# GpSimd in place of VectorE for the low halves of pieces 1 to 14 of the weights

## The chip, the cores and the metric

The kernel runs on one core of one Trainium2 chip. The metric is the time of one execution in device microseconds; three runs of the kernel before took 2193.1, 2188.76 and 2193.03 us, median 2193.03. The engines are named as in the profile: PE is TensorE (matmul), PEld its weight load, DVE is VectorE, ACT is ScalarE, POOL is GpSimd, SP is SyncE, which here issues most of the transfers.

## The reference, cut to what matters

One decoder layer over 512 positions of width 2048: adaLN modulation from a conditioning vector c, an input projection, an S5 mixer beside a dilated attention, an output projection and a SwiGLU channel mixer, in float32. The change lies in the first part:

```python
mod = (silu(c) @ w_mod + b_mod)                 # 6 blocks of 2048
h = rmsnorm(x, g_mix) * (1.0 + sc1) + sh1       # [512, 2048]
proj = h @ w_in                                 # [512, 4096] = u, q, k, v
```

## The kernel before

**Splits.** TensorE multiplies in fp32r. Each float32 operand is split in two: the high half is the value cast to fp32r, the low half is the value minus its high half. A product is three matmuls (`mm3`, lines 190 to 193): high by high, low by high and high by low. For weights a *piece* is 128 rows (one k tile) by 1024 columns of a matrix: SyncE loads it into `raw` (`load_piece`, 5 buffers), ScalarE casts it to `hi` (`split_piece`, line 161), and VectorE subtracts for `lo` (`split_lo`, line 165); `hi` and `lo` have 3 buffers each. A piece gives TensorE 24 matmuls: 8 blocks of 128 columns, 3 matmuls each, with a moving operand of 512 positions.

**Activations.** For each k tile, `h_make` forms the modulated input: VectorE multiplies (line 518, two halves of 256 positions), ScalarE adds the shift and casts to the high half (line 519, `hA` for k below 4 and `hB` above), VectorE forms the low half (line 523). It needs the modulation of tile k first: `gv` multiplies four 128x1024 parts of `w_mod` by the conditioning vector `cb` on VectorE (line 314, with an accumulated sum), and `h_mod` (lines 504 to 508) turns the sums into `gs` and `mod`. The parts of `w_mod` come through SyncE as well (`mraw`, 8 buffers in this phase).

**Order.** A list `prog` holds three products at the start: 4 pieces with k = 0 to 3 (partial q and k), 6 pieces with k = 0 to 5 (more of q and k), and 16 pieces with k = 0 to 15 (u). Pieces are counted through: 0 to 3, 4 to 9, 10 to 25. `run` walks the list; `need(i)` sees that pieces up to i are split, one or two ahead of TensorE; `pump` advances background work, among it `head_rest`, which makes the activations for k from 4 on. Each engine has one queue and works through it in order; the framework orders each queue by a priority, and splits have a raised one (`tc.high_priority(30)`). An instruction that waits holds all behind it on its engine. On SyncE the load of piece n+5 waits until piece n's `raw` has been read, and the loads of `mraw` queue behind it.

GpSimd has five small rows at the program's start and three transfers later; the first of these (`Kd<-s5z`, line 641) come at 182.9 us. All other splits, in the second half of the kernel too, are formed by ScalarE and VectorE.

## Time and profile before

| what | value |
|---|---|
| median of three runs | 2193.03 us |
| profiled execution, its own time | 2189.05 us |
| its span | 2187.2 us |
| PE busy | 2109.8 us (96%) |
| DVE busy | 1516.8 us (69%) |
| ACT busy | 849.6 us (39%) |
| POOL busy | 2.0 us, 7 instructions |
| L165, all low halves of weight pieces on DVE | 192 instructions, mean 1221 ns |
| L161, their high halves on ACT | 192 instructions, mean 1052 ns |

PE's share is near full over the whole span, but the first stages differ: there PE starts at 33.45 us and has gaps until 60 us. A busy share of a whole span therefore doesn't say what one of these stages is bound by. In the rows of a timeline the first number is the start, the second the duration; brackets give the idle time of the engine just before and what ended it. Starts of successive rows of one engine can lie closer than the duration, since instructions overlap at their ends. PEclk is the granted TensorE clock, 1.00 being full speed.

### The profile page before, as it was taken

The numbers are of one execution on the slowest core, as the hardware profiler recorded it, in microseconds if no ns is written. First come the engines' busy times: TensorE is split into PE (matmuls) and PEld (weight loads), VectorE is DVE, ScalarE is ACT, GpSimd is POOL, SyncE is SP. The second block draws the span as 40 slices with busy tenths as digits, with TensorE's granted clock in tenths as the row PEclk, the third lists the DMA queues.
The fourth block names the chain that finished last, engine by engine and source line by source line (L and its number), as shares of the span: only waits on it lengthen the run. The fifth ranks groups of instructions, "written<-read, shape, count | busy, mean of one in ns | idle before, by whom it ended". The sixth has DMA issues, their size and how long they took to land.

```text
span 2187.2 us, 32392 instructions
## 1 busy us (share of the span) xinstructions
PE 2109.8 (96%) x12800; PEld 1874.8 (86%) x12800; DVE 1516.8 (69%) x2216; ACT 849.6 (39%) x1209; POOL 2.0 (0%) x7
## 2 busy tenths in 40 slices
PE   6999999889999999999999999999999999999996
PEld 4778787767787778999999999999999888888885
DVE  7896886986888776687887888878887543242224
ACT  3432343257753253444444444444444111121111
POOL 0000000000000000000000000000000000000000
PEclk9999988999999999999999999999999999999998
DMA  9999785768887633343343333434435999655552
GB/s 344 339 357 174 215 248 197 238 210 296 299 284 249 219 114 97 130 144 123 135 138 132 128 135 131 143 123 136 138 132 217 323 320 327 204 195 194 193 173 77
DMA packets 212047, 435.92 MB, mean 199 GB/s; under 512 B 50676, under 2 KB 87924, under 8 KB 211896
## 3 DMA queue, kind: packets, MB, share of 16 engines
q1 hardware_dynamic: 211656, 433.13, 59.8%
q8 instruction: 101, 1.65, 0.3%
q0 software_dynamic: 240, 0.72, 0.1%
q14 instruction: 50, 0.41, 0.1%
HBM read 380.38 MB, written 53.41 MB: 198 GB/s over the span
## 4 chain that ended last, share of the span: by engine, by line
PE 73%; DVE 8%; DMA 3%; issue 1%; ACT 0%; DVEq 0%; SPq 0%; ACTq 0%
PE g L191 11%; PE g L193 11%; PE g L192 11%; PE y L1436 5%; PE y L1437 5%; PE y L1438 5%; PE z L1437 3%; PE x L1437 3%; PE x L1436 3%; PE z L1436 3%; PE x L1438 3%; PE z L1438 3%; DMA mraw<-in_w_mod 3%; DVE mraw L314 1%; DVE lo L165 1%
## 5 line engine op out<-in xcount | busy, mean ns | idle before, releaser
L165 DVE TENSOR_TENSOR lo<-raw,hi 128x1024 fp32r<-128x1024 f32 x192 | 234.2, 1221 | 323.8 <-ACT hi L161 323.7
L161 ACT CAST hi<-raw 128x1024 fp32r<-128x1024 f32 x192 | 201.6, 1052 | 557.4 <-PE g L192 356.3
L1167 ACT CAST hi<-raw 128x1024 fp32r<-128x1024 f32 x176 | 185.1, 1052 | 292.5 <-PE x L1437 125.4
L314 DVE SCALAR_TENSOR_TENSOR mraw<-mraw,cb 128x1024 f32<-128x1024 f32 x192 | 232.1, 1219 | 75.8 <-DMA mraw<-in_w_mod 75.6
L1169 DVE TENSOR_TENSOR lo<-raw,hi 128x1024 fp32r<-128x1024 f32 x176 | 215.1, 1223 | 90.2 <-ACT hi L1167 90.1
L191 PE MATMUL g<-f,hi 128*128 128x512 f32 x704 | 273.9, 389 | 0.0
L192 PE MATMUL g<-f,hi 128*128 128x512 f32 x704 | 273.9, 389 | 0.0
L193 PE MATMUL g<-f,lo 128*128 128x512 f32 x704 | 273.9, 389 | 0.0
L1167 ACT CAST hi<-s 128x1024 fp32r<-128x1024 f32 x120 | 126.3, 1053 | 165.0 <-PE y L1437 82.8
L1436 PE MATMUL y<-t,hi 128*128 128x256 f32 x640 | 179.8, 281 | 0.0
L1437 PE MATMUL y<-t,hi 128*128 128x256 f32 x640 | 179.8, 281 | 0.0
L1438 PE MATMUL y<-t,lo 128*128 128x256 f32 x640 | 179.8, 281 | 0.0
L1437 PE MATMUL x<-b,hi 128*128 128x256 f32 x640 | 179.8, 281 | 0.0
L1436 PE MATMUL x<-b,hi 128*128 128x256 f32 x640 | 179.8, 281 | 0.0
L1438 PE MATMUL x<-b,lo 128*128 128x256 f32 x640 | 179.8, 281 | 0.0
L1169 DVE TENSOR_TENSOR lo<-s,hi 128x1024 fp32r<-128x1024 f32 x120 | 146.5, 1221 | 16.3 <-ACT hi L1167 15.7
L193 PEld LDWEIGHTS g<-f,lo 128*128 128x128 f32 x704 | 132.1, 188 | 27.5
L191 PEld LDWEIGHTS g<-f,hi 128*128 128x128 f32 x704 | 132.1, 188 | 27.4
L192 PEld LDWEIGHTS g<-f,hi 128*128 128x128 f32 x704 | 132.1, 188 | 27.3
L191 PE MATMUL g<-hB,hi 128*128 128x512 f32 x288 | 115.6, 403 | 12.8 <-DVE rt L901 12.8
L1436 PEld LDWEIGHTS x<-b,hi 128*128 128x128 f32 x640 | 120.6, 188 | 0.0
L1437 PEld LDWEIGHTS x<-b,hi 128*128 128x128 f32 x640 | 120.6, 188 | 0.0
(321 smaller groups left out, 4935.4 us busy)
## 6 DMA issues: line engine op xcount, KB each, us to landing
mraw<-in_w_mod SPq DMA_DIRECT2D x192, 512.0 KB, 6.0
raw<-in_w_down SPq DMA_DIRECT2D x88, 512.0 KB, 3.9
f<-fd SPq DMA_DIRECT2D x88, 512.0 KB, 4.2
raw<-in_w_gate SPq DMA_DIRECT2D x80, 512.0 KB, 3.3
raw<-in_w_up SPq DMA_DIRECT2D x80, 512.0 KB, 3.8
raw<-in_w_in SPq DMA_DIRECT2D x64, 512.0 KB, 5.2
fd<-fo SPq DMA_DIRECT2D x40, 512.0 KB, 4.5
raw<-in_w_out SPq DMA_DIRECT2D x32, 512.0 KB, 5.4
```

The source lines that it names most:

```text
L161: ACT.copy(hi, p["raw"])
L165: tt(p["hl"][1], p["raw"], p["hl"][0].bitcast(F32), op=ALU.subtract)
L191: PE.matmul(ps, lhs[0], rhs[0], start=first, stop=False)
L192: PE.matmul(ps, lhs[0], rhs[1], start=False, stop=False)
L193: PE.matmul(ps, lhs[1], rhs[0], start=False, stop=last)
L314: stt(raw, raw, 1.0, cb[:, h * (D // 2):(h + 1) * (D // 2)], op0=ALU.mult, op1=ALU.mult, accum_out=macc[:, m, h:h + 1])
L1167: ACT.copy(hi, raw)
L1169: tt(lo, raw, hi.bitcast(F32), op=ALU.subtract)
L1436: PE.matmul(o, hi[:, sl], bh[:, k], start=f, stop=False, skip_group_check=True)
L1437: PE.matmul(o, hi[:, sl], bo[:, k], start=False, stop=False, skip_group_check=True)
L1438: PE.matmul(o, lo[:, sl], bh[:, k], start=False, stop=l, skip_group_check=True)
```

## The change

For pieces 1 to 14 of the first program the subtraction of the low half is issued on GpSimd; piece 0 and pieces from 15 on stay on VectorE. Before the second program (the channel mixer's last product) the limit is set to 0, so that nothing moves there.

```diff
     prog, pieces = [], []
+    LP = 14
     at = [0, 1, 0]
...
     def split_lo(p):
-        tt(p["hl"][1], p["raw"], p["hl"][0].bitcast(F32), op=ALU.subtract)
+        e = POOL if 0 < p["n_"] <= LP else DVE
+        e.tensor_tensor(p["hl"][1], p["raw"], p["hl"][0].bitcast(F32), op=ALU.subtract)
...
             with tc.high_priority(30):
+                pieces[at[0]]["n_"] = at[0]
                 split_lo(pieces[at[0]])
...
     prog.clear()
     pieces.clear()
+    LP = 0
     at[:] = [0, 0, 0]
```

Line numbers of the changed kernel are 2 or 3 higher here (165 becomes 167, 314 becomes 317, 518 becomes 521, 523 becomes 526).

VectorE's queue between the modulation of k=2 and the activations of k=3, before the change. `lo_344`, `lo_396`, `lo_448` and `lo_524` are the low halves of pieces 1 to 4, `st_413` belongs to k=2, `mraw_347` and those after it to k=3:

```order
L508 TENSOR_TENSOR gs<-gs,gb_164 128x1
L165 TENSOR_TENSOR lo_344<-raw_289,hi_343 128x1024
L518 SCALAR_TENSOR_TENSOR st_413<-vg,gs,rbc 128x256 x2
L165 TENSOR_TENSOR lo_396<-raw_291,hi_395 128x1024
L523 SCALAR_TENSOR_TENSOR hA_106<-st_413,mod,hA_105 128x256 x2
L165 TENSOR_TENSOR lo_448<-raw_293,hi_447 128x1024
L165 TENSOR_TENSOR lo_524<-raw_295,hi_523 128x1024
L314 SCALAR_TENSOR_TENSOR mraw_347,macc<-mraw_347,cb 128x1024
L314 SCALAR_TENSOR_TENSOR mraw_350,macc<-mraw_350,cb 128x1024
```

The same place of VectorE's queue in the changed kernel:

```order
L511 TENSOR_TENSOR gs<-gs,gb_164 128x1
L521 SCALAR_TENSOR_TENSOR st_413<-vg,gs,rbc 128x256 x2
L526 SCALAR_TENSOR_TENSOR hA_106<-st_413,mod,hA_105 128x256 x2
L317 SCALAR_TENSOR_TENSOR mraw_347,macc<-mraw_347,cb 128x1024
L317 SCALAR_TENSOR_TENSOR mraw_350,macc<-mraw_350,cb 128x1024
```

The four subtractions are gone from between the activations of k=2 and the modulation of k=3. GpSimd's queue before the change, from its last constant to the end:

```order
L1559 MEMSET const-uint8-127 128x1
L1565 UNCONDITIONAL_BRANCH
L641 DMA Kd<-s5z 112x512 x2
L1010 DMA mask<-in_km 128x512
L1565 UNCONDITIONAL_BRANCH
```

And in the changed kernel, from the same constant; the low halves of pieces 6 to 14 follow in the same form, and then the two transfers to `Kd`:

```order
L1563 MEMSET const-uint8-127 128x1
L1569 UNCONDITIONAL_BRANCH
L167 ISA
L167 TENSOR_TENSOR lo_344<-raw_289,hi_343 128x1024
L167 TENSOR_TENSOR lo_396<-raw_291,hi_395 128x1024
L167 TENSOR_TENSOR lo_448<-raw_293,hi_447 128x1024
L167 TENSOR_TENSOR lo_524<-raw_295,hi_523 128x1024
L167 TENSOR_TENSOR lo_530<-raw_306,hi_529 128x1024
```

The fourteen subtractions stand on GpSimd's queue now, behind one new ISA row. Each waits for its cast on ScalarE and, from piece 3 on, for TensorE to have left its buffer. On ScalarE's queue the casts of pieces 1 to 5 and of pieces 12 to 14 keep their places among the activations: the cast of piece 5 ahead of the activation of k=3, the cast of piece 13 behind three activations of k=7 and 8. On SyncE's queue the order stays, and the loads of pieces 6 to 19 wait for GpSimd's reading of the buffer where they waited for VectorE's.

## The prediction

> **What bounds the kernel now.** I read the stages first, then what TensorE waited for, then the rows of the engines that it waited for. The stages (busy time of each engine in six stretches):

> ```profile
> core 0: us, PE busy (x) PEld busy (x) DVE busy (x) ACT busy (x) POOL busy (x), PEclk, DMA share, GB/s
> 33.45:60.00 26.55, 20.29 (x75) 15.02 (x76) 24.95 (x51) 8.06 (x12) 0.00 (x0) 0.94 0.99 373
> 60.00:115.00 55.00, 55.00 (x236) 45.33 (x236) 46.76 (x112) 22.99 (x39) 0.00 (x0) 0.97 0.94 336
> 115.00:120.00 5.00, 3.84 (x16) 2.57 (x15) 5.00 (x9) 3.29 (x5) 0.00 (x0) 1.00 0.89 339
> 120.00:200.00 80.00, 80.00 (x355) 66.09 (x354) 75.18 (x174) 25.82 (x37) 1.19 (x2) 1.00 0.89 294
> ```

> The change ends with piece 14, whose low half is made at 118 us. From 60 us on TensorE is full, but for 1.16 us in 115 to 120; before that it is idle for 6.26 us while VectorE works for 24.95 of 26.55 us. So a faster VectorE can win back about 7.4 us and what the clock adds, and every microsecond that VectorE loses in these 85 us is near a gate of TensorE. TensorE's rows after a wait, in its timeline (start, duration, and in brackets the idle time and its releaser):

> ```profile
> 45.10 0.96 PE L193 MATMUL g<-hA,lo 128*128 128x512 f32 x3 [2.35 <-DVE lo L165]
> 58.60 1.22 PE L191 MATMUL g<-hA,hi 128*128 128x512 f32 x2 [3.67 <-ACT hA L519]
> 65.98 0.39 PE L191 MATMUL g<-hA,hi 128*128 128x512 f32 x1
> 116.05 0.50 PE L191 MATMUL g<-hA,hi 128*128 128x512 f32 x1 [0.27 <-ACT hi L161]
> 117.67 0.50 PE L193 MATMUL g<-hA,lo 128*128 128x512 f32 x1 [0.89 <-DVE lo L165]
> ```

> The first wait is for piece 1's low half, the second for the activations of k=3, the last two for piece 13. Piece 3 runs from 58.60 to 65.98, 7.38 us; the clock says why:

> ```profile
> 58.00:64.00 6.00, 5.40 (x13) 4.04 (x14) 5.93 (x12) 2.30 (x5) 0.00 (x0) 0.52 0.91 345
> 64.00:70.00 6.00, 6.00 (x28) 4.95 (x27) 3.06 (x5) 3.68 (x6) 0.00 (x0) 1.00 0.56 209
> ```

> After the wait of 3.67 us the granted clock was 0.52 for 6 us. By the stage from 120 to 200 a matmul takes 80/355 = 0.225 us at full clock, a piece of 24 takes 5.4 us, and the slow stretch cost 7.38 - 5.4 = 2.0 us. After the wait of 2.35 us three matmuls lasted 0.96 us, after the longer one two lasted 1.22: the shorter wait left the clock full.

> VectorE's timeline, with the low halves (L165) of pieces 1 to 5, then 6 to 12, and the rows that gate TensorE:

> ```profile
> 41.19 1.22 DVE L314 SCALAR_TENSOR_TENSOR mraw<-mraw,cb 128x1024 f32<-128x1024 f32 x1
> 43.81 1.23 DVE L165 TENSOR_TENSOR lo<-raw,hi 128x1024 fp32r<-128x1024 f32 x1
> 45.75 1.22 DVE L165 TENSOR_TENSOR lo<-raw,hi 128x1024 fp32r<-128x1024 f32 x1
> 47.68 1.22 DVE L165 TENSOR_TENSOR lo<-raw,hi 128x1024 fp32r<-128x1024 f32 x1
> 50.43 1.23 DVE L165 TENSOR_TENSOR lo<-raw,hi 128x1024 fp32r<-128x1024 f32 x1 [1.53 <-ACT hi L161]
> 51.57 1.22 DVE L314 SCALAR_TENSOR_TENSOR mraw<-mraw,cb 128x1024 f32<-128x1024 f32 x1
> 57.39 0.21 DVE L506 SCALAR_TENSOR_TENSOR mod<-macc,vec 128x1 f32<-128x1 f32 x1
> ...
> 84.08 1.23 DVE L165 TENSOR_TENSOR lo<-raw,hi 128x1024 fp32r<-128x1024 f32 x1 [1.31 <-ACT hi L161]
> 89.52 1.22 DVE L165 TENSOR_TENSOR lo<-raw,hi 128x1024 fp32r<-128x1024 f32 x1 [0.25 <-ACT hi L161]
> 96.47 1.22 DVE L165 TENSOR_TENSOR lo<-raw,hi 128x1024 fp32r<-128x1024 f32 x1
> 100.36 1.22 DVE L165 TENSOR_TENSOR lo<-raw,hi 128x1024 fp32r<-128x1024 f32 x1
> 113.23 0.88 DVE L518 SCALAR_TENSOR_TENSOR st<-vg,gs,rbc 128x256 f32<-128x256 f32 x2
> ```

> From the start at 50.43 to the next at 51.57 is 1.14 us: that is what a low half occupies of VectorE. And ScalarE's timeline, the casts to the high halves (L161) and the activations (L519):

> ```profile
> 39.80 1.98 ACT L161 CAST hi<-raw 128x1024 fp32r<-128x1024 f32 x2
> 46.29 1.03 ACT L161 CAST hi<-raw 128x1024 fp32r<-128x1024 f32 x1
> 54.74 1.04 ACT L161 CAST hi<-raw 128x1024 fp32r<-128x1024 f32 x1 [4.34 <-PE g L192]
> 57.64 0.91 ACT L519 ACTIVATE hA<-st,mod 128x256 fp32r<-128x256 f32 x2 [1.85 <-DVE mod L506]
> 77.74 1.05 ACT L161 CAST hi<-raw 128x1024 fp32r<-128x1024 f32 x1 [8.60 <-PE g L192]
> 78.69 1.31 ACT L519 ACTIVATE hB<-st,mod 128x256 fp32r<-128x256 f32 x3
> 113.75 1.31 ACT L519 ACTIVATE hB<-st,mod 128x256 fp32r<-128x256 f32 x3 [7.55 <-DVE st L518]
> 114.96 1.04 ACT L161 CAST hi<-raw 128x1024 fp32r<-128x1024 f32 x1
> ```

> **Gate 1** is the activation of k=3: VectorE's L506 at 57.39, ScalarE to 58.55, TensorE at 58.60. **Gate 2** is piece 13: its cast at 114.96 stands in ScalarE's queue behind activations that wait until VectorE's L518 at 113.23.

> **The change part by part.** VectorE loses 14 low halves, 14 x 1.14 = 16.0 us, all before 118 us. GpSimd gets them. Its queue was empty there (the page's busy tenths in 40 slices, then rows from the answers on `Kd` and of the timeline):

> ```profile
> POOL 0000000000000000000000000000000000000000
> L641 POOL DMA_DIRECT2D Kd<-s5z x2: 539/598/656, 182.9 to 183.5; - x2
> 182.87 1.22 DVE L314 SCALAR_TENSOR_TENSOR mraw<-mraw,cb 128x1024 f32<-128x1024 f32 x1
> ```

> The new queue starts with an ISA row that waits for nothing; it has 40 us until piece 1 and costs nothing. The two transfers behind the 14 rows, at 182.9, are 60 us clear of the last of them.

> How long does one of the 14 take there? No row has GpSimd at arithmetic on a tile. The nearest are the cast that reads one operand of the same size (39.80: 1.98 for two, 1.0 each) and VectorE's subtraction, 1.22. Both operands read one after the other is two such reads, 2.0 to 2.44. Below 1.0 nothing points, and above 5.4, a piece of TensorE, GpSimd could not keep up at all. I take 2.3, near two VectorE reads, since a subtraction has two operands. [...]

> The second unknown weighs more: how much of that time VectorE must stand still. Call it h. Almost all of VectorE's work beside these rows reads two operands from SBUF too (L314: mraw and cb; L518 and L523 as well). The one overlap in the trace, GpSimd's transfer at 182.9 beside L314 at 182.87 with its usual 1.22 us, reads no tile by GpSimd's arithmetic and says nothing. So h lies between 0 (side by side; less can't be) and 2.44 (in turns). I take turns, h = 2.3: two engines with the same two streams from the same tiles, and nothing in the trace that shows such streams beside each other.

> [...]

> *Gate 1.* Before 57.39 VectorE made pieces 1 to 4, 4 x 1.14 = 4.56, and stood 1.53 for piece 4's cast: 6.1 us go. Added are GpSimd's rows of pieces 1 to 5, whose casts end between 40.8 (just before VectorE's L314 at 41.19) and 55.8, so 5h. The gate moves by 5h - 6.1: at h = 2.3 by +5.4, to 64.0; it stands still at h = 1.2. TensorE's wait grows from 3.67 to some 9 us less what piece 2 starts later, and the slow clock stays, at the same 2.0 us. The earlier low half of piece 1 (40.8 + 2.3 = 43.1 for 45.0) is eaten by this longer wait.

> *Gate 2.* The activations of k=4 and 5 (78.69) stand behind a cast that had waited 8.60 us for TensorE, so around 80 us VectorE is at TensorE's +5.4 again, whatever it had gained or lost. From 84.08 to 113.23 it then had pieces 9 to 12, 4 x 1.14, and a wait of 0.25: 4.8 us go. Added are four or five GpSimd rows, 9.2 to 11.5: L518 comes 4.4 to 6.7 later still, take 5. TensorE's wait of 1.16 us grows by that. Then piece 13 itself: from cast to low half 2.3 in place of 1.22, where TensorE already waited 0.89: +1.1.

> Sum: 5.4 + 5 + 1.1 = **+11.5 us**. SyncE's queue: the load of piece n+5 now waits for GpSimd's row of piece n, with loads of mraw behind it. Piece 6's left after 45.03; with GpSimd at 43.1 to 43.5 it leaves earlier, so this costs nothing as long as GpSimd isn't more than a piece behind; if it is, it is the same lateness that the gates count. After 118 us nothing brings it back: TensorE is full from 120 to 200, and the chain of waits from there is

> ```profile
> PE 73%; DVE 8%; DMA 3%; issue 1%; ACT 0%; DVEq 0%; SPq 0%; ACTq 0%
> ```

> work that starts when TensorE's order gets there, so a shift is carried to the end one to one.

> **The rivals.** *Side by side* (the other side: faster; decides at h below 1.2). At h = 0 gate 1 for VectorE falls to 52.5, but ScalarE has the cast of piece 5 (54.74, which waits for TensorE's end of piece 2) ahead of k=3. Piece 1 resumes at 43.2, 1.9 earlier, piece 2 ends at 52.8 in place of 54.7, then cast 1.04 and activation 0.91: TensorE restarts at 54.8, 3.8 earlier, after a wait of 2.0, which by the row at 45.10 leaves the clock full: 2.0 more. With 1.16 at gate 2 that is -7.0, **2182**. For it: nothing forbids it in the trace. Against it: it needs h near 0, durations under 4 us and loads that keep up at a DMA share of 0.94 to 0.99, all at once.

> *Half and half*: h near 1.2, or side by side with a duration near 4.5 us (40.8 + 4.5 = 45.3, piece 1 as late as now). Gate 1 stands, gate 2 moves by 4 x 1.2 - 4.8 = 0, rows 13 and 14 cost up to 1: **2189 to 2190**.

> *GpSimd late*: VectorE's back-to-back work goes first and GpSimd waits for gaps. Then lo of piece 1 comes some 2 rows of VectorE (2.3 us) later, gate 1 shifts less (by 2 to 3) and gate 2 as above: +8, 2197. It lies within the forecast's range.

> That the change doesn't move the work is excluded: GpSimd's queue has the 14 rows.

> **How the numbers follow.** The profiled execution took 2189.05 us (span 2187.2 and 1.85 around it), the median of the three runs is 2193.03, and the runs stand at 2188.8 and 2193.1. Its own time plus 11.5 is 2200.5; the median of the changed kernel may be drawn from either level, so I name **2202**. Turns (with GpSimd late in it) get 0.67, side by side 0.20, half and half 0.13: slower needs one condition, faster three together. The range: 2189.05 + 5 to 2193 + 18 (14 rows at 2.44 against 1.14) for turns, 2194 to 2211, and one more if a wait at piece 13 longer than 3.67 us slows the clock again; reaching to side by side on the upper level, 2193 - 7, it is 2184 to 2212. About 0.2% (4.4 us) is what a measurement of this kernel can tell from no change: faster 0.20, same 0.13, slower 0.67.

> **What would show it.** Right: VectorE's rows of L314 and L518 beside a GpSimd row start late or last over 2 us; TensorE's wait at k=3 is 8 us or more; the one at piece 13 is 5 us or more; the U gemm ends some 11 us later. Wrong: L314 keeps its 1.22 us beside GpSimd's rows (h = 0), TensorE restarts at 55, and the clock keeps 1.00 from 55 to 64. If GpSimd's rows are far from 2.3 us, both gates scale with them.

## The result, and the profile after

| | before | after |
|---|---|---|
| median, runs on one chip | 2192.14 us (4 runs, 2188.76 to 2193.1) | 2206.16 us (4 runs, 2202.36 to 2209.88) |
| profiled execution, its own time | 2189.05 us | 2202.36 us |
| its span | 2187.2 us | 2200.6 us |

The ratio is 1.0063, with a 95% interval of 1.0048 to 1.0078: the change makes the kernel slower, by 14.0 us in the medians and 13.3 us between the profiled executions. The prediction had +11.5 us.

Page 1 of the profile after gives busy time, share of the span and instructions of each engine; from the costliest groups, `w_mod`'s multiplication on VectorE:

```profile
PE 2112.2 (96%) x12800; PEld 1875.8 (85%) x12800; DVE 1530.7 (70%) x2202; ACT 849.9 (39%) x1209; POOL 42.0 (2%) x21
L317 DVE SCALAR_TENSOR_TENSOR mraw<-mraw,cb 128x1024 f32<-128x1024 f32 x192 | 246.0, 1291 | 82.0 <-DMA mraw<-in_w_mod 81.6
```

VectorE lost 14 subtractions of 1.22 us, 17.1 us together, and yet is busy for 1530.7 us in place of 1516.8. So its other rows became 13.9 + 17.1 = 31.0 us longer: **2.2 us for each of the 14 GpSimd rows**. The largest part, 13.9 us, lies in L317 (246.0 us for 232.1 before).

The stages of the changed kernel (columns as before):

```profile
core 0: us, PE busy (x) PEld busy (x) DVE busy (x) ACT busy (x) POOL busy (x), PEclk, DMA share, GB/s
33.45:60.00 26.55, 20.08 (x72) 14.91 (x72) 26.26 (x37) 7.05 (x10) 14.45 (x5) 0.99 0.89 347
60.00:115.00 55.00, 49.34 (x204) 40.31 (x205) 46.73 (x90) 21.10 (x34) 17.68 (x7) 0.91 0.77 271
115.00:120.00 5.00, 4.66 (x21) 3.42 (x20) 4.89 (x12) 1.76 (x3) 0.00 (x0) 1.00 0.93 357
120.00:200.00 80.00, 73.45 (x317) 60.06 (x316) 76.88 (x152) 24.45 (x36) 9.07 (x4) 0.96 0.86 302
```

Until 60 us VectorE does 37 rows in 26.26 us, where it did 51 in 24.95. TensorE has holes in stages in which it was full: 5.66 us between 60 and 115, 6.55 between 120 and 200. Its rows after a wait, from the timeline of the changed kernel (start, duration; in brackets the idle time before and its releaser):

```profile
63.59 1.65 PE L194 MATMUL g<-hA,hi 128*128 128x512 f32 x3 [7.79 <-ACT hA L522]
107.49 0.50 PE L194 MATMUL g<-hA,hi 128*128 128x512 f32 x1 [2.07 <-ACT st L541]
117.65 0.50 PE L194 MATMUL g<-hA,hi 128*128 128x512 f32 x1 [0.34 <-ACT st L541]
126.73 0.50 PE L194 MATMUL g<-hA,hi 128*128 128x512 f32 x1 [2.65 <-ACT hi L162]
131.36 0.79 PE L196 MATMUL g<-hA,lo 128*128 128x512 f32 x1 [3.89 <-POOL lo L167]
```

The first row is gate 1, 5.0 us later than at 58.60. The last two are piece 13, its high half and its low half. The two in between are a place that was free before. VectorE's timeline shows how gates 1 and 2 came late:

```profile
41.18 3.40 DVE L317 SCALAR_TENSOR_TENSOR mraw<-mraw,cb 128x1024 f32<-128x1024 f32 x1
44.52 3.40 DVE L317 SCALAR_TENSOR_TENSOR mraw<-mraw,cb 128x1024 f32<-128x1024 f32 x1
51.30 3.41 DVE L317 SCALAR_TENSOR_TENSOR mraw<-mraw,cb 128x1024 f32<-128x1024 f32 x1
54.76 2.21 DVE L507 SCALAR_TENSOR_TENSOR gs<-macc,vec 128x1 f32<-128x1 f32 x1
57.00 2.26 DVE L511 TENSOR_TENSOR gs<-gs,gb 128x1 f32<-128x1 f32 x1
62.38 0.22 DVE L509 SCALAR_TENSOR_TENSOR mod<-macc,vec 128x1 f32<-128x1 f32 x1
...
123.92 0.88 DVE L521 SCALAR_TENSOR_TENSOR st<-vg,gs,rbc 128x256 f32<-128x256 f32 x2
127.89 1.22 DVE L317 SCALAR_TENSOR_TENSOR mraw<-mraw,cb 128x1024 f32<-128x1024 f32 x1
129.03 3.35 DVE L167 TENSOR_TENSOR lo<-raw,hi 128x1024 fp32r<-128x1024 f32 x1
```

L317 takes 1.22 us beside anything else and 3.40 us here, and rows of one element per partition (L507, L511) take 2.2 us where they took 0.2: five rows, one for each of the pieces 1 to 5. The modulation of k=3 (L509) comes at 62.38 for 57.39. GpSimd's own rows, from its timeline:

```profile
40.90 5.94 POOL L167 TENSOR_TENSOR lo<-raw,hi 128x1024 fp32r<-128x1024 f32 x2 [40.45 <-ACT hi L162]
50.74 8.51 POOL L167 TENSOR_TENSOR lo<-raw,hi 128x1024 fp32r<-128x1024 f32 x3 [3.91 <-DMA mraw<-in_w_mod]
73.08 2.40 POOL L167 TENSOR_TENSOR lo<-raw,hi 128x1024 fp32r<-128x1024 f32 x1 [13.83 <-ACT hi L162]
126.76 4.55 POOL L167 TENSOR_TENSOR lo<-raw,hi 128x1024 fp32r<-128x1024 f32 x1 [13.92 <-ACT hi L162]
```

One takes 2.40 us when it gets through at once. The last is piece 13's: 4.55 us. From 126.70 to 129.03 VectorE went from row to row without a gap, and its subtraction at 129.03 is the first that is stretched: GpSimd stood for some 2.2 us first, and VectorE after that. ScalarE's timeline has the link in the new place at 107.49 and the cast of piece 13:

```profile
106.06 0.91 ACT L522 ACTIVATE hB<-st,mod 128x256 fp32r<-128x256 f32 x2 [3.48 <-DVE mod L509]
106.87 2.02 ACT L541 COPY st<-g 128x512 f32<-128x512 f32 x4
125.65 1.03 ACT L162 CAST hi<-raw 128x1024 fp32r<-128x1024 f32 x1
```

The copies that empty PSUM (L541) stand in ScalarE's queue behind an activation that waits for VectorE's modulation, and TensorE waits for the copies. Last, the granted clock around the two long waits:

```profile
64.00:70.00 6.00, 6.00 (x16) 4.68 (x16) 5.89 (x13) 2.35 (x4) 0.00 (x0) 0.53 0.84 282
127.00:127.60 0.60, 0.47 (x2) 0.03 (x1) 0.60 (x3) 0.60 (x2) 0.60 (x1) 1.00 1.03 423
127.61:134.40 6.79, 3.04 (x7) 2.46 (x8) 6.79 (x5) 1.36 (x2) 6.79 (x2) 0.50 0.89 282
```

Half clock after k=3 was there before as well. The stretch from 127.61 on is new; it begins only 0.14 us into the wait of 3.89 us, so it follows the wait of 2.65 us that ended at 126.73.

### The profile page after: what moved, and what is told of

It is laid out like the page before. It is cut to its first block, busy times and chain, and to the rows that moved or that the text cites. A ratio compares the mean times of both kernels' runs of the same rounds, so it can differ in the third digit from the quotient of the medians.

```text
span 2200.6 us, 32417 instructions
## 1 busy us (share of the span) xinstructions
PE 2112.2 (96%) x12800; PEld 1875.8 (85%) x12800; DVE 1530.7 (70%) x2202; ACT 849.9 (39%) x1209; POOL 42.0 (2%) x21
## 4 chain that ended last, share of the span: by engine, by line
PE 72%; DVE 8%; DMA 4%; issue 1%; ACT 0%; SPq 0%; DVEq 0%; ACTq 0%
PE g L196 11%; PE g L194 11%; PE g L195 11%; PE y L1440 5%; PE y L1442 5%; PE y L1441 5%; PE x L1441 3%; PE z L1442 3%; PE z L1441 3%; PE x L1440 3%; PE z L1440 3%; PE x L1442 3%; DMA mraw<-in_w_mod 2%; DVE mraw L317 1%; DVE lo L167 1%
## 5 line engine op out<-in xcount | busy, mean ns | idle before, releaser
L167 DVE TENSOR_TENSOR lo<-raw,hi 128x1024 fp32r<-128x1024 f32 x178 | 219.8, 1237 | 310.2 <-ACT hi L162 301.6
L317 DVE SCALAR_TENSOR_TENSOR mraw<-mraw,cb 128x1024 f32<-128x1024 f32 x192 | 246.0, 1291 | 82.0 <-DMA mraw<-in_w_mod 81.6
L1172 DVE TENSOR_TENSOR lo<-raw,hi 128x1024 fp32r<-128x1024 f32 x176 | 215.1, 1223 | 89.7 <-ACT hi L1170 89.5
L1440 PEld LDWEIGHTS y<-t,hi 128*128 128x128 f32 x640 | 120.6, 188 | 0.5 <-issue 0.5
L1440 PEld LDWEIGHTS x<-b,hi 128*128 128x128 f32 x640 | 120.6, 188 | 0.0
```

What stands on the lines that cost most here:

```text
L167: e.tensor_tensor(p["hl"][1], p["raw"], p["hl"][0].bitcast(F32), op=ALU.subtract)
L317: stt(raw, raw, 1.0, cb[:, h * (D // 2):(h + 1) * (D // 2)], op0=ALU.mult, op1=ALU.mult, accum_out=macc[:, m, h:h + 1])
L1172: tt(lo, raw, hi.bitcast(F32), op=ALU.subtract)
L1440: PE.matmul(o, hi[:, sl], bh[:, k], start=f, stop=False, skip_group_check=True)
```

## The experiments

The theory, "turns": while a GpSimd row reads SBUF, VectorE's rows stand still, for about the row's length. The rival, "lateness": VectorE loses nothing, and the low halves merely come later, from a slower engine with a queue of its own. All comparisons of single executions go by three points of TensorE's timeline: the restart at k=3, the first matmul of u, and the first matmul of the product after u (first with `hi` in the place of `hA`). Whole times serve only where there are many runs, since 23 runs of the kernel before lay between 2188.56 and 2198.16 us on one chip; on the chip of the kernels pieces 1 to 4, subtraction unread, copy unread and fill it ran once, 2197.96 us.

| kernel | k=3 | u starts | u ends | u ends, against before | time, us |
|---|---|---|---|---|---|
| before | 58.60 | 99.30 | 188.07 | | 2189.05 |
| after | 63.59 | 104.57 | 203.17 | +15.1 | 2202.36 |
| pieces 1 to 4 | 62.60 | 103.55 | 191.76 | +3.7 | 2192.35 |
| pieces 5 to 14 | 62.61 | 103.07 | 200.17 | +12.1 | 2206.03 |
| subtraction unread | 68.77 | 113.30 | 210.71 | +22.6 | 2219.65 |
| copy unread | 63.50 | 103.69 | 197.43 | +9.4 | 2199.76 |
| fill | 58.74 | 99.12 | 190.25 | +2.2 | 2194.13 |
| pieces 28 to 41 | 60.16 | 101.20 | 189.98 | +1.9 | 2194.69 |

The last row is also a measure of scatter: that kernel has no GpSimd row before 192 us, so its +1.9 is what one execution differs from another up to there. Its source is in the trace: behind the wait for piece 1's low half the clock was 0.50 from 45.60 to 49.02 us, where in the execution of before it was 1.00.

**Pieces 1 to 4 alone.**

```diff
-    LP = 14
+    LP = 4
```

> Only pieces 1 to 4 on GpSimd. Turns (VectorE stands still for as long as a GpSimd row lasts): gate 1 moves by 4 x 2.3 - 6.1 = +3.1 us, TensorE restarts for k=3 near 61.7 us after a wait of 6 to 7 us, gate 2 hardly changes, the whole +3 to +4 us. Rival, lateness (what costs is only that a low half is ready 2.4 us after its cast and not 1.2): pieces 1 to 4 are not late for TensorE, so 0 or a small gain.

TensorE's row at k=3 of this kernel, from its timeline,

```profile
62.60 1.65 PE L194 MATMUL g<-hA,hi 128*128 128x512 f32 x3 [5.07 <-ACT hA L522]
```

and the row of VectorE's timeline just ahead of its modulation of k=3:

```profile
60.25 1.22 DVE L167 TENSOR_TENSOR lo<-raw,hi 128x1024 fp32r<-128x1024 f32 x1
```

Four GpSimd rows at 2.2 us, less the 6.1 us gone, would be +2.7; but piece 5's low half, which VectorE keeps here, now stands ahead of the modulation, at 60.25, where it stood behind it before (57.52 against 57.39). With its 1.14 us the sum is +3.8, and +4.0 was measured. u ends +3.7: what happens at this gate is carried through, and the remaining 11.4 us of the change come from pieces 5 to 14.

**The subtraction twice.** VectorE keeps the low halves; GpSimd makes those of pieces 1 to 14 once more, into a tile that nothing reads. No low half can come late from a slower engine here; what is left of lateness is that GpSimd's reading holds `raw` and `hi` longer.

```diff
     def split_lo(p):
         tt(p["hl"][1], p["raw"], p["hl"][0].bitcast(F32), op=ALU.subtract)
+        if 0 < p["n_"] <= LP:
+            POOL.tensor_tensor(scr, p["raw"], p["hl"][0].bitcast(F32), op=ALU.subtract)
```

> VectorE keeps all its low halves, GpSimd repeats the subtraction of pieces 1 to 14 into a tile that nobody reads. Turns: nothing is taken from VectorE and 14 x 2.3 = 32 us of standing still are added; k=3 restarts TensorE at 68 to 70 us, the whole is +20 to +28 us, and VectorE's rows of 128x1024 beside a GpSimd row last 3.4 us. Lateness: the low halves come as early as before, so 0 to +2 us.

TensorE's long waits in its timeline, and the row of VectorE's timeline beside the first subtraction:

```profile
49.43 1.65 PE L197 MATMUL g<-hA,lo 128*128 128x512 f32 x3 [6.02 <-DVE lo L166]
68.77 1.22 PE L195 MATMUL g<-hA,hi 128*128 128x512 f32 x2 [7.81 <-ACT hA L524]
137.36 0.80 PE L195 MATMUL g<-hA,hi 128*128 128x512 f32 x1 [4.96 <-ACT hi L162]
```

```profile
41.20 3.42 DVE L319 SCALAR_TENSOR_TENSOR mraw<-mraw,cb 128x1024 f32<-128x1024 f32 x1
```

+22.6 us from rows whose result nobody uses, and VectorE's row itself lasts 2.2 us longer (3.42 for 1.22), where a late buffer would only start it later. Turns holds; lateness alone falls.

**One operand in place of two.** The same, with a copy of `hi` in place of the subtraction.

```diff
+        if 0 < p["n_"] <= LP:
+            POOL.tensor_copy(scr, p["hl"][0].bitcast(F32))
```

> VectorE keeps all its low halves, GpSimd copies the high halves of pieces 1 to 14 into a tile that nobody reads: one operand in place of two. If any reading by GpSimd stops VectorE: each row stops it for its own length (1 to 2.4 us), the whole is +8 to +20 us. If only GpSimd rows with two operands do: VectorE's rows stay at 1.22 us and the whole is within 2 us of before.

GpSimd's group (busy time and mean ns, then idle time and its releaser), and two rows of VectorE's timeline beside the first two copies:

```profile
L168 POOL COPY scr<-hi 128x1024 f32<-128x1024 f32 x14 | 22.0, 1575 | 104.8 <-ACT hi L162 104.5
```

```profile
41.16 2.06 DVE L319 SCALAR_TENSOR_TENSOR mraw<-mraw,cb 128x1024 f32<-128x1024 f32 x1
43.15 2.04 DVE L319 SCALAR_TENSOR_TENSOR mraw<-mraw,cb 128x1024 f32<-128x1024 f32 x1
```

Reading one operand stops VectorE too, for 0.83 us (2.05 less 1.22), and u ends 9.4 us later. A copy that gets through at once takes 1.04 us (94.01), a subtraction 2.40: both times VectorE's standstill is 0.2 us less than GpSimd's row. So in these two kernels the price follows the length of that row.

**Writing alone.** VectorE keeps the low halves; GpSimd first fills the same tile with zeros.

```diff
+        if 0 < p["n_"] <= LP:
+            POOL.memset(p["hl"][1].bitcast(F32), 0.0)
```

> VectorE keeps all its low halves, GpSimd first fills the low buffers of pieces 1 to 14 with zeros: it writes and reads nothing. Turns by reading: VectorE's rows beside the fills stay at 1.22 us and the whole is within 2 us of before. Rival (any work of GpSimd on SBUF stops VectorE): VectorE's rows stretch beside the fills, by the fills' own length, and the whole is +5 to +15 us.

A fill in GpSimd's timeline, the row of VectorE's timeline beside it, and TensorE's two waits at piece 13, with the windows behind them:

```profile
42.25 0.96 POOL L167 MEMSET lo<- 128x1024 f32 x1 [39.68 <-PE g L197]
```

```profile
42.37 1.22 DVE L318 SCALAR_TENSOR_TENSOR mraw<-mraw,cb 128x1024 f32<-128x1024 f32 x1
```

```profile
116.25 0.50 PE L195 MATMUL g<-hA,hi 128*128 128x512 f32 x1 [0.65 <-ACT hi L162]
118.28 0.79 PE L197 MATMUL g<-hA,lo 128*128 128x512 f32 x1 [1.29 <-DVE lo L168]
```

```profile
118.00:120.00 2.00, 1.72 (x4) 1.43 (x5) 2.00 (x4) 0.49 (x1) 0.00 (x0) 0.57 1.04 424
120.00:122.00 2.00, 2.00 (x6) 1.55 (x6) 2.00 (x4) 0.00 (x0) 0.00 (x0) 0.58 1.04 395
```

VectorE keeps its 1.22 us, none of its rows beside the other fills is longer than usual (all 192 of L318 have a mean of 1219 ns, the same as before), k=3 stays where it was, and u starts on time. So here it is GpSimd's reading that stops VectorE (by 2.2 us with two operands, 0.83 with one), not its writing. The +2.2 at the end of u, a little over the 2 us expected at most, are 0.78 us of longer waits at piece 13 (0.65 + 1.29 for 0.27 + 0.89) and the half clock behind them; whether the waits grew by the fills or by scatter isn't told apart.

**Pieces 5 to 14 alone.**

```diff
-        e = POOL if 0 < p["n_"] <= LP else DVE
+        e = POOL if 4 < p["n_"] <= LP else DVE
```

> Only pieces 5 to 14 on GpSimd. Turns: gate 1 changes by piece 5 at most (0 to +2 us), gate 2 as in the changed kernel, +7 to +10 us; with the run of pieces 1 to 4 the two parts add up to about the change's +13. Lateness: about +2 us, piece 13's low half alone.

TensorE's waits in its timeline, and VectorE's row behind k=3's:

```profile
62.61 0.80 PE L194 MATMUL g<-hA,hi 128*128 128x512 f32 x1 [5.74 <-ACT hA L522]
123.70 0.50 PE L194 MATMUL g<-hA,hi 128*128 128x512 f32 x1 [1.94 <-ACT hi L162]
128.32 0.80 PE L196 MATMUL g<-hA,lo 128*128 128x512 f32 x1 [3.89 <-POOL lo L167]
```

```profile
58.94 2.55 DVE L521 SCALAR_TENSOR_TENSOR st<-vg,gs,rbc 128x256 f32<-128x256 f32 x1
```

The expectation for k=3 was missed: +4.0. Half of it is one stretched row (2.55 for 0.48), the price of piece 5 at gate 1, which the expectation put too low. The other half was there before GpSimd's first row at 57.81: piece 4 was cast at 51.29, for 49.34 before, as in the kernel of pieces 28 to 41 (50.91), which at that time differs from before in nothing. In both executions the clock was 0.50 just ahead of that cast, here from 46.06 to 49.48, so the other half is the scatter named above. From k=3 to the end of u 8.1 us more are lost, within the 7 to 10 expected for gate 2. At piece 13 the last wait is the same 3.89 us as in the full change, without pieces 1 to 4. The two parts, 3.7 and 12.1, make 15.8 against 15.1 for the whole, within the scatter.

**The same rows where VectorE has time.** Fourteen pieces of the products behind u.

```diff
-        e = POOL if 0 < p["n_"] <= LP else DVE
+        e = POOL if 27 < p["n_"] <= LP else DVE
```

(with `LP = 41`)

> The 14 low halves of pieces 28 to 41 on GpSimd in place of 1 to 14 (about 200 to 275 us), where VectorE's rows of low halves are each preceded by a wait of 3 to 4 us until about 230 us. Turns: where VectorE waits anyway a standstill costs nothing, so 0 until 230 us, and up to +5 us after it, where VectorE is busy again. If GpSimd is a loss wherever it is used: +10 us or more.

A GpSimd row and TensorE's longest wait behind one, from the timelines:

```profile
202.27 2.39 POOL L167 TENSOR_TENSOR lo<-raw,hi 128x1024 fp32r<-128x1024 f32 x1 [3.01 <-ACT hi L162]
```

```profile
234.13 0.79 PE L195 MATMUL g<-lo,hB 128*128 128x512 f32 x1 [2.66 <-POOL lo L167]
```

Five rows between 192 and 216 cost TensorE no wait. From 230 on, where VectorE is busy again, they do. The low half is waited for longer (2.66 us for 0.74), and the clock is at 0.50 from 234 to 240. Four waits for VectorE's rows of the S5 mixer are new, 1.80, 1.49, 1.12 and 0.93 us; the first of them, and the stretch in the kernel before and in this one:

```profile
255.12 1.03 PE L750 MATMUL m<-Q,E 128*128 128x16 f32 x8 [1.80 <-DVE s5X L779]
```

```profile
230.00:300.00 70.00, 69.06 (x365) 58.70 (x365) 63.14 (x117) 30.88 (x67) 0.00 (x0) 0.98 0.78 231
230.00:300.00 70.00, 61.22 (x299) 50.15 (x300) 63.51 (x92) 25.24 (x56) 23.77 (x9) 0.93 0.68 202
```

TensorE gets through 66 matmuls fewer and is idle for 8.8 us in place of 0.9: more than the 5 us expected at most from 230 on. It makes this good behind it: from 300 to 340 us this kernel runs 251 matmuls at a clock of 1.00, the kernel before 188 at 0.74. Why the clock differs there stays open. The single time, 2194.69, lies within those of before, so the whole time shows neither gain nor loss, but these rows are not free where VectorE is busy.

**VectorE relieved without GpSimd.** If gate 1 is VectorE's order, and the slow clock its consequence, then the low half of piece 4, which is needed only after k=3, should go behind the modulation of k=3. No piece goes to GpSimd; `m3` holds the instruction L506 of k=3.

```diff
-            with tc.high_priority(30):
+            with tc.high_priority(30), (tc.issue_after(m3[0].ins) if m3 and at[0] in (4,) else nullcontext()):
                 split_lo(pieces[at[0]])
```

> No GpSimd: the low half of piece 4, on VectorE, is placed behind the modulation of k=3 (1.14 us of work and 1.53 us of waiting leave the path to gate 1). By the account of gate 1: TensorE restarts when ScalarE has cast piece 5 and made the activation, near 56.7 us for 58.6, after a wait of 1.9 us, which leaves the clock full (2 us more): -3.9 us in all, about 2188. Rival (the wait is bound by loads or by something else than VectorE's order): 0.

TensorE's row at k=3, and the window behind it:

```profile
56.82 1.45 PE L192 MATMUL g<-hA,hi 128*128 128x512 f32 x5 [1.72 <-ACT hA L522]
```

```profile
58.00:64.00 6.00, 6.00 (x28) 4.94 (x27) 5.51 (x10) 3.79 (x7) 0.00 (x0) 1.00 1.03 409
```

The wait is 1.72 us for 3.67 and the clock stays full: 28 matmuls from 58 to 64, for 13 before. u ends at 185.00, 3.1 us earlier. Over 12 runs of this kernel and 23 of the kernel before on the same chip the median is 2187.54 against 2193.41 us, ratio 0.998 (0.9968 to 0.9992). The 5.9 us between the medians are more than the 3.9 expected and the 3.1 at the end of u; the rest is not explained.

**And ScalarE's cast of piece 5 behind the activation of k=3.** `a3` holds that activation.

```diff
+                with (tc.issue_after(a3[0].ins) if a3 and at[2] == 5 else nullcontext()):
+                    split_piece(pieces[at[2]])
```

> As the kernel with piece 4 placed later, and ScalarE casts piece 5 behind the activation of k=3. TensorE restarts near 55.7 us, -4.9 us in all, about 2187; if VectorE's modulation of k=3 is the last to end (54.7 and then the activation) it is the same as with piece 4 alone.

TensorE's row at k=3 in its timeline:

```profile
56.10 1.42 PE L193 MATMUL g<-hA,hi 128*128 128x512 f32 x5 [1.05 <-ACT hA L523]
```

0.7 us earlier again. Over 12 runs the median is 2187.15 us, ratio 0.9974 (0.9963 to 0.9984): faster than both the kernel before and the changed one, with no work taken from VectorE. Whether it beats the former version is not told by these intervals, which overlap.

## Why the prediction was right

The likeliest case came, turns, and in it each term can be set beside its measurement, with the rows from which the measurement comes in the last column:

| step | predicted | measured | read from |
|---|---|---|---|
| h, VectorE's standstill per GpSimd row | 2.3 | 2.2 | 31.0 us in 14 rows |
| gate 1 | +5.4 | +5.0 | 63.59 for 58.60 |
| slow clock after it | no change | +0.3 | u starts at 104.57 for 99.30 |
| gate 2 | +5 | +4.8 | 2.07 + 0.34 + 2.65 for 0.27 |
| low half of piece 13 | +1.1 | +3.0 | 3.89 for 0.89 |
| slow clock after that | left to the range | +1.4 | 131.36 to 137.89 (first `hB` of u) for 117.67 to 122.79 |
| TensorE's restarts in u | not in the sum | +0.6 | what remains of 15.1: 0.3 at each of the two waits in the new places |
| from there to the end | one to one | -1.7 | +15.1 at the end of u, +13.4 in the span |
| sum | +11.5 | +13.4 | span 2200.6 for 2187.2 |

*h.* The choice of turns was the step that decided the sign. It was the author's estimate: the two engines have the same two streams, and no row of the kernel before bore it out. Subtraction and copy with unread results, and the fill, show it apart from everything else: in them reading by GpSimd stopped VectorE and writing didn't, with VectorE's row of 128x1024 at 3.42 us for 1.22 beside the subtraction, 2.05 beside the copy, 1.22 beside the fill. That GpSimd's row would be two reads of an operand long was guessed from other engines, and the copy (1.04) and the subtraction (2.40) bear it out.

*Gate 1.* 5h - 6.1 with h = 2.2 is +4.9; L509 came 5.0 us later. TensorE's wait there, 7.79 us, is a little under the 8 named as a sign. The kernel with pieces 1 to 4 alone bears the formula out with four rows.

*Gate 2.* VectorE's L521 came at 123.92 for 113.23, +10.7, of which 5.3 was TensorE's own shift at the start of u: 5.4 more, where 4.4 to 6.7 was forecast. But it was not all paid at piece 13. Of TensorE's 5.06 us of waits, 2.41 were paid at the copies from PSUM on ScalarE (L541), which the prediction did not have among what stands behind a late activation. The 2.07 us are the same lateness of VectorE, met earlier, and so the sum held; the copy behind the other 0.34 us had waited, by the profile, for a transfer of `part`.

*Piece 13's low half* is the term that was mis-sized. The prediction gave GpSimd its lone duration there, 2.3 for 1.22, though turns can go either way: with VectorE's rows back to back, GpSimd stood as well, and the row took 4.55 us for 2.40. What the rival "GpSimd late" feared for piece 1 happened here; at piece 1 the row took 2.61 us (its first of the two in 5.94), and that rival's smaller shift at gate 1 didn't come. The clock was halved again, the case named in the range, though not by the length of this wait: it was down from 127.61 on, when TensorE had stood for 0.14 us of the 3.89.

*One to one.* Between the end of u and the end of the span 1.7 us came back, and the step that nothing brings a shift back did not hold. Most of it moved at one place: up to 222 us TensorE is 15.0 us behind, at 240 us 12.7, and 0.7 are lost again after it. There TensorE waits in both kernels, 2.49 and 0.74 us before, 1.06 and 1.49 after, and only before was the clock halved behind it (0.57 from 231 to 235, for 1.00 from 246 to 250). Some of the other kernels here have the half clock there and some don't, so this can't be put down to the change. It stays open.

*The clock.* The prediction read a wait of 2.35 us as one that leaves the clock full and one of 3.67 us as one that halves it. In the kernel of pieces 28 to 41 a wait of 1.98 us at the same place halved it, so the length of a wait didn't decide this here (see the last section). The forecast did not suffer: the term was taken as unchanged at gate 1, and there it changed by 0.3 us.

*Luck.* Piece 13's low half, the slow clock and the restarts were short by 3.9 us together, and the sum is short by only 1.9 because 1.7 us came back that it did not foresee. The lower end of the range, 2184, does not follow from its own 2193 - 7, which is 2186; nothing hung on it. The rows listed as the low halves of pieces 1 to 5 and 6 to 12 are those of 1 to 4 and 9 to 12, the ones the sums use.

*The rivals.* Side by side (2182) needed h below 1.2, half and half (2190) h near 1.2; with 2.2 measured both are out. What they asked for is what the version with piece 4 put off does: gate 1 earlier, a shorter wait, and the clock full.

## What to carry to other kernels

Work given to GpSimd was not free for VectorE here: beside a GpSimd row that read two tiles VectorE's row took 2.2 us longer (3.40 for 1.22), beside one that read a single tile 0.83 us longer, and its usual 1.22 us beside one that only wrote. So a 1.14 us subtraction moved away cost VectorE 2.2 us elsewhere. Before an engine is relieved, look for work on it that stands ahead of the gate and is needed after it: to put off one low half and one cast won 0.26%, where moving fourteen lost 0.63%. Where VectorE waited anyway, the same rows cost TensorE no wait (five rows between 192 and 216 us). And keep TensorE's waits short and apart: 1.94 us of them close together (the fills) and 1.98 us (pieces 28 to 41) brought half clock here, and half clock cost 1.4 us (after piece 13) to 2.0 us (k=3 before).
